# A two-layer hybrid decoder trunk: the low parts of the weight tiles by an accumulating transfer

## Chip, cores and metric

The kernel runs on one core of a Trainium2 chip. The metric is the device time of one execution in microseconds. Two runs of the kernel before took 1311.83 and 1311.68 us, median 1311.76 us.

## What is computed

A sequence of 16 meta tokens and 512 input tokens of width 1024 goes through two layers in float32. Each layer has a mixer (one input projection of 26 column tiles, three kinds of heads side by side, one output projection of 8 column tiles) and a gated MLP (an up projection of 44 column tiles, a causal convolution of width 3, a down projection). Cut to what matters here:

```python
for l in range(DEPTH):                      # DEPTH = 2
    h = h + hybrid_mixer(rmsnorm(h, norm_mix_g[l]), w_in[l], ..., w_out[l], cos, sin)
    h = h + conv_glu_ffn(rmsnorm(h, norm_ffn_g[l]), ffn_w_up[l], ffn_conv_w[l],
                         ffn_conv_b[l], ffn_w_down[l])
return rmsnorm(h, final_norm_g)[:, N_META:]
```

## The kernel before

The residual stream lives in on-chip memory with features on partitions: `hT` is 128 x 8 x 528 (8 feature tiles, 528 tokens). Tokens are worked in two halves of 264 (256 to 258 in parts of the last layer).

Every projection is done with split operands. A float32 value is cut into a high part, rounded to the matmul's own float type, and a low part, the difference. For one column tile of a weight and one token half, `product` (L234) issues for each of the 8 contraction tiles (7 in some down projections) three products into one accumulator: high weight by high activation, high weight by low activation, low weight by high activation. That is 24 products per half. The activations are split by `split` (L304: ACT rounds, VectorE subtracts).

The weights come as a stream of 204 tiles, listed in `units` (L181 to L201) in the order of their use. A tile is 128 x 1024 float32, 512 KB. `fetch` (L205) has SP load it into a `raw` buffer, of which there are three. `prep` (L214) makes the parts: ACT rounds `raw` into `wh` (L222), VectorE subtracts `wh` from `raw` into `wl` (L223), and then the load of the tile two places on is issued (L226). `wh` and `wl` have four buffers each (`wpool`, L91). `pop` (L228) is called when the work on tile i begins and prepares tile i + 3. The parts of the first four tiles are made by code of their own at the start (`cut`, `hi`, `lo`, L974 to L991), half tile by half tile in places.

`run_units` (L245) walks through the tiles of a projection. Most tiles are worked alone: both token halves, then the next tile. At some places four tiles form a block that is worked token half by token half: first halves of all four, then second halves of all four, so that the second half of the inputs can be late. The blocks are the first four tiles of each input projection, both halves of the 8 tiles of each output projection, the first four of the first up group of each layer, and the 8 tiles of each layer's last down group.

The order on TensorE (PE) and SP is the order of the code, written by hand. ACT, VectorE (DVE) and GpSimd (POOL) are ordered by a scheduler that estimates when each instruction can go; every engine then works its list strictly in that order. The mixers' own products are put between the projection products by generators with estimated distances (`tick`, L128). POOL does only small memsets: the pads of new tiles, among them the first two columns of each up projection tile (L882).

Names in rows: `mm` are the accumulators of projections, `mx` those of mixers and norms; `xh`, `xl` and `ah`, `al` are the parts of activations; L305 and L306 are `split`; L320 and L316 take squares for a norm; L884 and L886 move an up projection's result out of the accumulator; L894 is its convolution, L901 a sigmoid, L855 a residual add.

Of the kernel before, what the change touches and what calls it, by code (L numbers as in the profile page):

```python
# [9 lines left out]
F32 = mybir.dt.float32  # L10
F32R = mybir.dt.float32r
I32 = mybir.dt.int32
AF = mybir.ActivationFunctionType
# [21 lines left out]
# distances, in us of the PE's work, between dependent products of the mixers and norms  # L35
# [28 lines left out]
# columns of the packed masks  # L64
# [5 lines left out]
# columns of the packed per-layer parameters  # L70
# [6 lines left out]
C_LAM, C_LB = 0, 2 * DEPTH        # of the parameters that are worked on first  # L77
NPRE = C_LB + 4 * DEPTH

# columns of the packed float constants  # L80
# [5 lines left out]
def hybrid_trunk_kernel(ctx, tc, x, w_in, w_out, w_up, w_down, par, pre_in, lru_w, kon, msk, rope, out):  # L86
# [21 lines left out]
    # Estimated PE time, for the distance between dependent products of a mixer.  # L108
    clk = [0.0]
    live = []          # [generator, earliest clock, key]  # L110
# [103 lines left out]
    def prep(upto):  # L214
        while n_prep[0] <= min(upto, len(units) - 1):
            i = n_prep[0]
            fetch(i)
            r, kn = raws.pop(i)
            wh = wpool.tile([P, KD * P], F32R, tag="wh", name=nm("wh"))
            wl = wpool.tile([P, KD * P], F32R, tag="wl", name=nm("wl"))  # L220
            n = kn * P
            S.copy(wh[:, 0:n], r[:, 0:n])  # L222
            V.tensor_tensor(wl[:, 0:n], r[:, 0:n], wh[:, 0:n].bitcast(F32), op=ALU.subtract)  # L223
            ready[i] = (wh, wl)
            n_prep[0] += 1
            fetch(i + 2)  # L226
# [18 lines left out]
    def run_units(todo, xs, halves, ks=None, first=0, last=0, between=None, late=0, joint=0):  # L245
        """todo: (needs, evac(i, t0, n, ps), after()) per unit. The first `first` and the last
        `last` units go token half by token half; the last `late` of the contraction tiles come
        after the others of all of the first units' first half."""
# [60 lines left out]
    accs = {}  # L309

    def norm_sq(k, t0, n, apart=False):
        """Adds the squares of one tile of h to the sums of its token half; those of the last may stay apart."""
        if k == 0 or apart and k == KD - 1:
            a = half("acc", 3) if k == 0 else half("hs")
            accs.setdefault(t0, []).append(a)
            S.activation(a[:, 0:n], hT[:, k, t0:t0 + n], AF.Square)  # L316
            return
        a = accs[t0][0]
        sq = half("hs")
        S.activation(sq[:, 0:n], hT[:, k, t0:t0 + n], AF.Square)  # L320
        V.tensor_tensor(a[:, 0:n], a[:, 0:n], sq[:, 0:n], op=ALU.add)

    def warm(n):
        """Keeps the array busy while it has nothing else to do: its clock rises with its use."""
        if n:
            ps = mx()
            for _ in range(n):
                PE.matmul(ps[:, 0:P], ones, ones, start=True, stop=True)  # L328

    def rstd(terms, n):  # L330
        """1 / sqrt of the mean square of n tokens, worked out with the tokens on partitions."""
        m = 2 if n <= 2 * P else 3
        w = n // m
        ps = mx()
        for a, t in enumerate(terms):
            for i in range(m):
                mm(ps[0:w, 8 * i + a:8 * i + a + 1], t[:, i * w:(i + 1) * w], mean0[:, 0:1])
        ss, sd, rs = (big("sm", 9, (P, 20)) for _ in range(3))
        V.tensor_reduce(ss[0:w, 0:m], ps[0:w, 0:8 * m].rearrange("p (i a) -> p i a", a=8)[:, :, 0:len(terms)],
                        axis=AX.X, op=ALU.add)  # L340
        S.activation(sd[0:w, 0:m], ss[0:w, 0:m], AF.Sqrt, bias=eps[0:w], scale=1.0)
        V.reciprocal(rs[0:w, 0:m], sd[0:w, 0:m])
        dg = half("dg", 1)
        V.tensor_tensor(dg[0:w, 0:n].rearrange("p (i t) -> p i t", t=w), ident[0:w, 0:w].unsqueeze(1).to_broadcast([w, m, w]),
                        rs[0:w, 0:m].unsqueeze(2).to_broadcast([w, m, w]), op=ALU.mult)
        return dg, w

    def spread(dgw, n):
        """The factors of the tokens, the same on every partition."""
        dg, w = dgw  # L350
        ps = mx()
        mm(ps[:, 0:n], ones[0:w, :], dg[0:w, 0:n])
        return ps[:, 0:n]
# [23 lines left out]
    def pieces(t0, n):  # L377
        """Splits a token range at chunk bounds: (first chunk, chunks, offset in the chunk, tokens, start)."""
# [23 lines left out]
    def hgrn_evac(l, h, d):  # L402
# [7 lines left out]
        def q(i, t0, n, ps):  # L410
            sg = half("hs")
            S.activation(sg[:, 0:n], ps[:, 0:n], AF.Sigmoid)
            # the factor 1 - lb of k rides on q: both meet only in products over the same feature
# [11 lines left out]
    # Scores of a chunk, sum_d q_t k_s prod_{s<r<=t} f_r, level by level: for blocks of h tokens,  # L425
    # A holds q times the decay from the start of its block and B k times the decay to the end of
    # its block (both products of factors in [0, 1]), and T the decay over whole blocks. Neighbour
    # blocks 2i, 2i+1 meet as A x B; two levels at a time share one stationary B.
    def hgrn(l, h, d, on):
# [15 lines left out]
        def blocks(x, n, hb, which):  # L445
            """The even (0) or odd (1) ones of each chunk's first 2n blocks of hb tokens."""
            return (x[:, :, 0:2 * n * hb].rearrange("p c (n two h) -> p c n two h", two=2, h=hb)[:, :, :, which, :])
# [4 lines left out]
        def grow(x, n, hb, t, which):  # L452
            """x of the even / odd blocks times the decay over their odd / even neighbours."""
# [10 lines left out]
        def put(cs, k, src, n, hb, m):  # L464
            """Keeps what the mask allows of the scores of the odd ones of 2n blocks of hb tokens."""
# [15 lines left out]
        # levels 2 and 4  # L481
# [27 lines left out]
        # levels 8 and 16  # L509
# [20 lines left out]
        # levels 32 and 64; the last block of 32 has 16 tokens  # L530
# [36 lines left out]
        # tokens on partitions: the sums of the norm are over the free axis, and the factors per partition  # L567
# [155 lines left out]
    def lru(l, j, xp, on):  # L723
# [16 lines left out]
        # with u = -log(a) / 2 and h = tanh(u): a = 2 / (1 + h) - 1, sqrt(1 - a^2) = 2 sqrt(h) / (1 + h)  # L740
# [38 lines left out]
    def layer(l):  # L779
# [71 lines left out]
        # output projection and residual, then the second norm  # L851
# [13 lines left out]
        # gated MLP  # L865
# [5 lines left out]
        def up_pair(j):  # L871
            us = {}

            def ev(key, m):
                """Keeps the product u, and starts the convolution with its last tap."""
# [76 lines left out]
    with tc.manual_schedule(engines={mybir.EngineType.PE, mybir.EngineType.SP}):  # L952
# [5 lines left out]
        # the first call loads the table of the square root, which holds the squares too  # L958
# [15 lines left out]
        def cut(i):  # L974
            """Starts the split of weight tile i; hi and lo go half by half."""
# [219 lines left out]
```

## Time and profile before

| | |
|---|---|
| median of two runs | 1311.76 us |
| span of the profiled execution | 1310.1 us |
| PE busy | 1295.4 us |
| VectorE busy | 836.7 us |
| ACT busy | 652.9 us |
| POOL busy | 9.3 us |
| transfers, share of the 16 DMA engines | 27.2% in the loads' queue |

The profile shows one execution. Its span runs from the first to the last instruction; the times of the two runs are 1.6 to 1.7 us longer than that span. Busy times of engines overlap. A busy share tells how much an engine works, not what it makes others wait for; that is read from the waits and from the chain of work that ended last, which is followed back from the last instruction to what released each step. Line numbers are those of the kernel before; those of the kernel after are higher by one from L224 on.

### The profile page before, as it was taken

The page shows a single profiled execution, that of the slowest core. Times are in us where ns is not written, and L with a number is a line of the kernel's source. Part 1 is how long each engine was busy: PE and PEld are TensorE (multiplying, and loading weights), DVE is VectorE, ACT ScalarE, POOL GpSimd, SP SyncE. Part 2 cuts the span into 40 slices and gives each one's busy share as a digit, 9 for nine tenths or more (in the row PEclk, how much of TensorE's full clock was granted, in tenths as well). Part 3 has the DMA queues.
Part 4 walks back from the last instruction along what each step waited for, and adds up shares of the span by engine and source line. Part 5 has one row for each costly group of instructions (what it writes and reads, how often), then busy time and mean ns, then how long its engine had stood idle before and what let it go on. Part 6 is the DMA issues. An engine that isn't in the chain of part 4 may idle for free.

```text
span 1310.1 us, 25008 instructions
## 1 busy us (share of the span) xinstructions
PE 1295.4 (99%) x10312; PEld 1271.0 (97%) x10312; DVE 836.7 (64%) x1588; ACT 652.9 (50%) x1314; POOL 9.3 (1%) x99
## 2 busy tenths in 40 slices
PE   9999999999999999999999999999999999999997
PEld 9999999999999999999999999999999899989997
DVE  7987676477654664466488767754866456636654
ACT  6665555256533552455366645553655245425541
POOL 0000000000000000000000000000000000000000
PEclk8999999999999999999999999999999999999999
DMA  5222312223332323323222222122332333332221
GB/s 194 97 78 63 98 57 74 81 66 113 89 90 97 97 74 103 94 86 98 65 88 75 65 66 97 62 68 66 104 106 86 94 97 92 85 113 87 91 65 66
DMA packets 36082, 114.22 MB, mean 87 GB/s; under 512 B 3840, under 2 KB 8448, under 8 KB 35968
## 3 DMA queue, kind: packets, MB, share of 16 engines
q1 hardware_dynamic: 34816, 110.46, 27.2%
q10 hardware_dynamic: 1152, 2.16, 0.5%
q8 instruction: 81, 1.33, 0.4%
q14 instruction: 33, 0.27, 0.1%
HBM read 110.51 MB, written 2.10 MB: 86 GB/s over the span
## 4 chain that ended last, share of the span: by engine, by line
PE 93%; DVE 3%; ACT 2%; DMA 1%; issue 0%; SPq 0%; DVEq 0%; ACTq 0%
PE mm L115 85%; PE mx L115 7%; PE mx L122 1%; DVE t L443 1%; DMA raw<-in_w_in_dram 0%; DVE sc L467 0%; DMA mk<-in_msk_dram 0%; DVE t L746 0%; ACT sc L550 0%; DVE wl L223 0%; DVE t L933 0%; ACT wh L222 0%; DVE hT L855 0%; DVE rr L443 0%; PE mx L328 0%
## 5 line engine op out<-in xcount | busy, mean ns | idle before, releaser
L115 PE MATMUL mm<-xh,wh 128*128 128x264 f32 (+2 forms) x2240 | 648.0, 289 | 0.0
L115 PE MATMUL mm<-xh,wl 128*128 128x264 f32 (+2 forms) x2240 | 634.9, 283 | 0.0
L115 PE MATMUL mm<-xl,wh 128*128 128x264 f32 (+2 forms) x2240 | 634.3, 283 | 0.0
L115 PEld LDWEIGHTS mm<-xh,wh 128*128 128x128 f32 x2240 | 422.6, 189 | 2.4 <-issue 2.0
L115 PEld LDWEIGHTS mm<-xl,wh 128*128 128x128 f32 x2240 | 422.1, 188 | 2.6 <-issue 1.9
L115 PEld LDWEIGHTS mm<-xh,wl 128*128 128x128 f32 x2240 | 422.7, 189 | 0.1
L223 DVE TENSOR_TENSOR wl<-raw,wh 128x1024 fp32r<-128x1024 f32 (+1 forms) x200 | 240.4, 1203 | 170.7 <-ACT wh L222 170.1
L222 ACT CAST wh<-raw 128x1024 fp32r<-128x1024 f32 (+1 forms) x200 | 206.6, 1033 | 245.0 <-PE mm L115 244.9
L115 PE MATMUL mm<-ah,wh 128*128 128x264 f32 (+3 forms) x848 | 253.9, 299 | 0.0
L115 PE MATMUL mm<-al,wh 128*128 128x264 f32 (+3 forms) x848 | 252.8, 298 | 0.0
L115 PE MATMUL mm<-ah,wl 128*128 128x264 f32 (+3 forms) x848 | 252.4, 298 | 0.0
L115 PEld LDWEIGHTS mm<-al,wh 128*128 128x128 f32 x848 | 159.6, 188 | 5.0
L115 PEld LDWEIGHTS mm<-ah,wl 128*128 128x128 f32 x848 | 159.7, 188 | 4.9
L115 PEld LDWEIGHTS mm<-ah,wh 128*128 128x128 f32 x848 | 159.6, 188 | 4.9
L894 DVE SCALAR_TENSOR_TENSOR t<-t,pr,t 128x528 f32<-128x528 f32 (+1 forms) x176 | 133.1, 757 | 3.0
L886 ACT ACTIVATE t<-mm,pr 128x264 f32<-128x264 f32 (+1 forms) x176 | 101.2, 575 | 0.0
L884 ACT COPY t<-mm 128x264 f32<-128x264 f32 (+2 forms) x176 | 65.2, 371 | 56.8 <-PE mm L115 56.8
L776 DVE TENSOR_TENSOR hT<-hT,mm 128x264 f32<-128x264 f32 (+1 forms) x48 | 24.7, 515 | 76.6 <-PE mm L115 76.6
L901 ACT ACTIVATE t<-t 128x528 f32<-128x528 f32 (+1 forms) x44 | 28.1, 639 | 86.3 <-DVE t L894 86.2
L855 DVE TENSOR_TENSOR hT<-hT,mm 128x264 f32<-128x264 f32 (+2 forms) x64 | 26.3, 424 | 56.0 <-PE mm L115 56.0
L320 ACT ACTIVATE hs<-hT 128x264 f32<-128x264 f32 (+2 forms) x52 | 21.3, 419 | 60.0 <-DVE hT L855 58.5
L902 DVE TENSOR_TENSOR t<-t,t 128x528 f32<-128x528 f32 (+1 forms) x44 | 30.8, 701 | 31.2 <-ACT t L901 31.0
(189 smaller groups left out, 1058.5 us busy)
## 6 DMA issues: line engine op xcount, KB each, us to landing
raw<-in_w_up_dram SPq DMA_DIRECT2D x88, 512.0 KB, 3.6
raw<-in_w_in_dram SPq DMA_DIRECT2D x52, 512.0 KB, 3.6
raw<-in_w_down_dram SPq DMA_DIRECT2D x32, 448.0 KB, 3.3
raw<-in_w_out_dram SPq DMA_DIRECT2D x16, 512.0 KB, 3.6
raw<-in_w_down_dram SPq DMA_DIRECT2D x16, 512.0 KB, 3.6
hT<-in_x_dram SPq DMA_DIRECT2D x4, 528.0 KB, 5.6
t<-in_rope_dram ACTq DMA_DIRECT2D x8, 264.0 KB, 3.2
out_dram<-t SPq DMA_DIRECT2D x8, 256.0 KB, 2.2
```

The source lines that it names most:

```text
L115: PE.matmul(o, a, b, start=start, stop=stop)
L122: PE.transpose(o, a, ident[0:n, 0:n])
L222: S.copy(wh[:, 0:n], r[:, 0:n])
L223: V.tensor_tensor(wl[:, 0:n], r[:, 0:n], wh[:, 0:n].bitcast(F32), op=ALU.subtract)
L320: S.activation(sq[:, 0:n], hT[:, k, t0:t0 + n], AF.Square)
L776: V.tensor_tensor(hT[:, m, t0:t0 + n], hT[:, m, t0:t0 + n], ps[:, 0:n], op=ALU.add)
L855: V.tensor_tensor(hT[:, m, t0:t0 + n], hT[:, m, t0:t0 + n], ps[:, 0:n], op=ALU.add)
L884: S.copy(u[:, 2 + t0:2 + t0 + n], ps[:, 0:n])
L886: S.activation(c[:, o - c0:t0 + n - c0], ps[:, o - t0:n], AF.Identity, bias=pr[l][:, C_FB + m:C_FB + m + 1], scale=pr[l][:, w + 2:w + 3])
L894: V.scalar_tensor_tensor(c[:, 0:cn], u[:, i + c0:i + c0 + cn], pr[l][:, w + i:w + i + 1], c[:, 0:cn], op0=ALU.mult, op1=ALU.add)
L901: S.activation(sg[:, 0:cn], c[:, 0:cn], AF.Sigmoid)
L902: V.tensor_tensor(c[:, 0:cn], c[:, 0:cn], sg[:, 0:cn], op=ALU.mult)
```

## The change

In `prep`, VectorE's subtraction goes. ACT makes a second pass over the raw tile and writes it to `wl` negated, rounded by the type of `wl` as `wh` is. Then POOL issues a transfer from `raw` to `wl`, both in on-chip memory, that adds its source to what stands in the destination, so that `wl` ends as raw minus rounded raw. The diff also strips comments and docstrings, which changes no instruction.

```diff
             S.copy(wh[:, 0:n], r[:, 0:n])
-            V.tensor_tensor(wl[:, 0:n], r[:, 0:n], wh[:, 0:n].bitcast(F32), op=ALU.subtract)
+            S.activation(wl[:, 0:n], r[:, 0:n], AF.Copy, scale=-1.0)
+            G.dma_start(wl[:, 0:n], r[:, 0:n], accum_op=ALU.add)
             ready[i] = (wh, wl)
```

The first four tiles keep VectorE's subtraction. The order on PE and SP is the same as before, but what each waits for is not: PE's third product of a contraction tile now waits for the transfer, and a raw buffer may be loaded again only when the transfer that reads it has landed. On ACT, POOL and VectorE the scheduler has made a new order.

On ACT, just before the first singles of layer 0's input projection, the copies of the fifth and sixth tile stand like this before:

```order
L222 CAST wh_261<-raw_259 128x1024
L827 COPY t_318<-mm_448 128x264
L404 ACTIVATE t_321<-mm_449 128x264
L405 ACTIVATE t_322<-mm_449 128x264
L727 ACTIVATE t_642<-t_318,pr_78 128x528
L222 CAST wh_332<-raw_265 128x1024
```

and after:

```order
L222 CAST wh_261<-raw_259 128x1024
L828 COPY t_319<-mm_451 128x264
L405 ACTIVATE t_322<-mm_452 128x264
L406 ACTIVATE t_323<-mm_452 128x264
L728 ACTIVATE t_646<-t_319,pr_78 128x528
L223 ACTIVATE wl_262<-raw_259 128x1024
L413 ACTIVATE hs_600<-mm_575 128x264
L222 CAST wh_333<-raw_266 128x1024
```

The negated copy (L223) of the fifth tile stands behind four instructions that follow its rounding copy. On ACT at the change from layer 0's output projection to its up projection, the second and third tile of the up projection's first block are treated like this before (`xh` is the norm's rounding):

```order
L222 CAST wh_3270<-raw_3204 128x1024
L305 CAST xh<-hs_3402 128x264
L305 CAST xh<-hs_3406 128x264
L305 CAST xh<-hs_3410 128x264
L305 CAST xh<-hs_3414 128x264
L222 CAST wh_3305<-raw_3239 128x1024
```

and after:

```order
L222 CAST wh_3301<-raw_3234 128x1024
L306 CAST xh<-hs_3435 128x264
L306 CAST xh<-hs_3439 128x264
L306 CAST xh<-hs_3443 128x264
L306 CAST xh<-hs_3447 128x264
L223 ACTIVATE wl_3302<-raw_3234 128x1024
L222 CAST wh_3337<-raw_3270 128x1024
```

The second tile's negated copy comes after four of the norm's roundings, and the third tile's rounding copy one instruction later. POOL, where the up projection of layer 0 begins, has only memsets before:

```order
L882 MEMSET t_3532 128x2
L882 MEMSET t_3583 128x2
L882 MEMSET t_3653 128x2
L882 MEMSET t_3689 128x2
L882 MEMSET t_3857 128x2
```

and after, transfers (L224) with memsets between them:

```order
L224 DMA wl_3338<-raw_3270 128x1024
L224 DMA wl_3535<-raw_3306 128x1024
L883 MEMSET t_3618 128x2
L883 MEMSET t_3689 128x2
L883 MEMSET t_3726 128x2
L224 DMA wl_3572<-raw_3342 128x1024
L224 DMA wl_3624<-raw_3539 128x1024
```

POOL's queue is worked in this order, so a transfer goes when the memsets ahead of it have gone.

## Rows read from the trace of the kernel before

**Rows 1.** The page, part 1: busy time, share of the span, instructions.

```profile
PE 1295.4 (99%) x10312; PEld 1271.0 (97%) x10312; DVE 836.7 (64%) x1588; ACT 652.9 (50%) x1314; POOL 9.3 (1%) x99
```

**Rows 2.** The chain that ended last: shares by engine; pieces (start us, us, what).

```profile
PE 93%; DVE 3%; ACT 2%; DMA 1%; issue 0%; SPq 0%; DVEq 0%; ACTq 0%
...
281.70 0.87 PE mx L115 x12
...
284.59 367.89 PE mm L115 x3030
```

**Rows 3.** Waits of PE's weight loads: us in total, times, longest us.

```profile
PEld mx L115 <- DVE dg L344: 3.0, 2, 1.6
...
PEld mx L115 <- ACT bt L556: 1.3, 2, 0.8
```

**Rows 4.** Groups by line: busy us, mean ns of one | idle before.

```profile
L223 DVE TENSOR_TENSOR wl<-raw,wh 128x1024 fp32r<-128x1024 f32 (+1 forms) x200 | 240.4, 1203 | 170.7 <-ACT wh L222 170.1
L222 ACT CAST wh<-raw 128x1024 fp32r<-128x1024 f32 (+1 forms) x200 | 206.6, 1033 | 245.0 <-PE mm L115 244.9
...
L886 ACT ACTIVATE t<-mm,pr 128x264 f32<-128x264 f32 (+1 forms) x176 | 101.2, 575 | 0.0
L884 ACT COPY t<-mm 128x264 f32<-128x264 f32 (+2 forms) x176 | 65.2, 371 | 56.8 <-PE mm L115 56.8
```

**Rows 5.** Waits of all engines: us in total, times, longest us.

```profile
POOL t L882 <- DVE t L894: 269.9, 20, 95.8
```

**Rows 6.** Queues (packets, MB, share) and issues (KB each, median us to landing).

```profile
q1 hardware_dynamic: 34816, 110.46, 27.2%
...
raw<-in_w_up_dram SPq DMA_DIRECT2D x88, 512.0 KB, 3.6
...
hT<-in_x_dram SPq DMA_DIRECT2D x4, 528.0 KB, 5.6
```

**Rows 7.** Stretches: us; PE, PEld, DVE, ACT, POOL busy; clock, DMA share, GB/s.

```profile
10.00:14.30 4.30, 3.13 (x12) 2.93 (x13) 3.72 (x11) 3.40 (x9) 0.00 (x0) 0.52 1.06 391
...
60.00:180.00 120.00, 119.41 (x963) 116.64 (x962) 89.97 (x210) 67.09 (x163) 1.46 (x13) 1.00 0.26 79
```

**Rows 8.** Timeline, 34 to 41 us: start us, us, instruction, idle before.

```profile
34.33 1.05 ACT L222 CAST wh<-raw 128x1024 fp32r<-128x1024 f32 x1 [1.77 <-PE mm L115]
...
36.11 0.84 ACT L727 ACTIVATE t<-t,pr 128x528 f32<-128x528 f32 x1
...
40.55 1.06 ACT L222 CAST wh<-raw 128x1024 fp32r<-128x1024 f32 x1 [1.43 <-PE mm L115]
```

**Rows 9.** Timeline, 243 to 254 us.

```profile
243.11 1.05 ACT L222 CAST wh<-raw 128x1024 fp32r<-128x1024 f32 x1 [1.84 <-PE mm L115]
...
245.45 0.33 SPq L210 DMA_DIRECT2D raw<-in_w_out_dram  x1
...
251.90 1.05 ACT L222 CAST wh<-raw 128x1024 fp32r<-128x1024 f32 x1 [1.55 <-PE mm L115]
...
252.85 0.42 ACT L320 ACTIVATE hs<-hT 128x264 f32<-128x264 f32 x1
```

**Rows 10.** Timeline, 270 to 280 us.

```profile
270.67 1.05 ACT L222 CAST wh<-raw 128x1024 fp32r<-128x1024 f32 x1 [2.00 <-PE mm L115]
271.62 1.35 ACT L305 CAST xh<-hs 128x264 fp32r<-128x264 f32 x4
...
276.47 0.28 PE L115 MATMUL mm<-xh,wh 128*128 128x264 f32 x1
```

**Rows 11.** Timeline of ACT, 290 to 312 us.

```profile
292.49 1.05 ACT L222 CAST wh<-raw 128x1024 fp32r<-128x1024 f32 x1 [1.26 <-PE mm L115]
...
295.41 1.05 ACT L222 CAST wh<-raw 128x1024 fp32r<-128x1024 f32 x1 [1.12 <-PE mm L115]
...
298.52 0.65 ACT L901 ACTIVATE t<-t 128x528 f32<-128x528 f32 x1
```

## The prediction, made before the change was run

> **What bounds the kernel now.** I read the busy shares first [rows 1]: TensorE (PE) works 1295.4 of 1310.1 us, VectorE (DVE) 836.7, ScalarE (ACT) 652.9, GpSimd (POOL) 9.3. Then the chain of work that ended last [rows 2]: 93% PE, and its longest unbroken piece is 3030 products in 367.89 us. That is 0.1214 us a product, so a weight tile's half of the tokens (8 contraction tiles by 3 products) lasts 24 x 0.1214 = 2.91 us and a whole tile 5.83 us. Then the waits of PE's weight loads [rows 3]: the longest for other engines come to 3.0 and 1.3 us in all. PE is idle for 14.7 us in total, so an edit that only relieves VectorE has at most about 15 us to win, and the edit's cost is whatever new waiting it puts in front of PE. The question is therefore not how busy the engines are but when a tile's low part is there.
>
> **What goes and what comes.** The subtraction is 200 x 1203 ns = 240.4 us of VectorE [rows 4]; it goes, and VectorE falls to about 596 us. It is not what PE waits for, so I credit nothing; the bounds are 0 and 5 us, the waits of rows 3 together with a little of what stands on DVE in the chain. In its place ACT makes a second pass over the tile, priced as the rounding copy of the same shape: 200 x 1033 ns = 207 us [rows 4], ACT to about 860 us or 66%. In the mixers of layer 0 ACT has 67 of 120 us [rows 7], to which some 14 tiles add 15; VectorE there has 90 and loses 17. These two I set against each other, with 5 us either way. POOL issues 200 transfers. Its in-order queue holds the memsets of the new tiles in between, so a late memset would hold a transfer; in the trace they wait for their buffers up to 95.8 us [rows 5], but go as soon as these are free, well before they are used, so nothing is charged.
>
> The third part decides: an accumulating transfer of 512 KB within the on-chip memory. Call L the time from its issue to its landing. No such transfer is in the trace. The lower end is a plain load of the same bytes, 3.6 us [rows 6]. The upper end is two such loads one after the other, 7.2 us, since source and destination both have to be fetched; the first loads of the program, which run several at a time, land after 5.6 us for about the same bytes. Between the ends: the loads' queue takes 27.2% of 1310.1 us [rows 6], 356 us, for 211 loads' worth of bytes (110.46 MB / 0.524 MB), so 1.69 us of the DMA engines per load. So a landing of 3.6 is 1.9 fixed and 1.69 moving; with both operands moving it is 1.9 + 3.4 = 5.3 alone, and 7.0 if a weight load shares the engines. I take the middle, L = 6.2, and stretch a load that runs beside it by 0.85.
>
> **Where L is covered and where not.** There are four buffers for the low parts. In a run of single tiles the buffer for tile i+3 comes free as tile i starts, so three tiles, 17.5 us, lie between release and need. ACT needs some 3.1 of these (copy, an eviction, negated copy), so L could be 14 before PE waits; nothing is lost there. Where four tiles are worked token half by token half, all four buffers are held until the second halves end, one every 2.91 us, and the next tile is needed three halves, 8.7 us, after the first release. Each such place, read from the ACT timeline:
>
> Start [rows 8]. The fifth tile's copy begins at 34.33; four evictions follow, the last ending at 36.95, and the negated copy stands behind them in ACT's new order, ending at 38.0. The block ends at 40.55 (where the copy of tile eight is released), the low part is read by the third product, so at 40.8. Cover 2.8, loss L - 2.8 = 3.4 us.
>
> Second block of the output projection [rows 9]. The release of its first buffer is at 243.11; copy and negated copy end at 245.2; the need is at 251.9, so up to L = 6.7 it is covered. The fourth tile is another matter. There are three buffers for the raw tiles, and its load was issued at 245.45, when the first tile's subtraction had read the buffer. Now the buffer is held until the accumulate has landed: 245.2 + L, load 3.6 + 0.85, copy 1.05, a square 0.42, negated copy 1.05, and L again: 252.2 + 2L, against a need at 251.9 + 3 x 2.91 + 0.2 = 260.9. Loss 2L - 8.7 = 3.7 us. On SP only further loads stand behind the waiting one.
>
> First block of the up projection [rows 2, 10]. The second tile's copy starts at 270.67, the four roundings of the norm (1.35) now stand between it and the negated copy, which ends at 274.0; the block starts at 276.47, so the need is at 276.47 + 2.91 + 0.2 = 279.6. Cover 5.6, loss 0.6 us. The third and fourth are needed more than 2.91 us apart, since PE breaks off at 281.70 for the norm's products and comes back to long work only at 284.59; by the same steps they are covered somewhat longer, to about 6.
>
> First singles after it [rows 11]. The first has its copy at 292.49 and its negated copy, behind an eviction (0.37 + 0.58 [rows 4]), ends at 295.35; the block ends three halves after 292.49, need at 301.4: covered to 6.1. The second: its copy at 295.41, then an eviction, a table load, a sigmoid that ends at 299.2, the next tile's copy (1.05), an eviction (0.95) and a rounding of the sigmoid's shape (0.65); with these the negated copy ends at about 302.5, need 5.83 later at 307.3. Cover 4.8, loss 1.4 us.
>
> The last three places together lose 5.7 us. They come once with layer 0's output projection, once where layer 0's down projection meets layer 1's input projection, and once with layer 1's output projection: 17.1. The last down projection has a second block only: 3.7. With the start, 17.1 + 3.7 + 3.4 = 24.2 us. The profiled execution would span 1310.1 + 24.2 = 1334.3; the two timed runs (median 1311.76) lie 1.7 above the span of before, so 1336. Per microsecond of L the loss changes by 15 (one at the start, 2 x 4 in the second blocks, 3 + 3 in the other places): at 5.3 it is 12 us, at 7.2 about 39. At 3.6 only the start is left, 0.8.
>
> What the loss leaves out is PE's clock. It is granted at 1.00 (2.4 GHz) from 60 to 180 us, where PE hardly idles, and at 0.52, near the 1.2 GHz level, from 10.0 to 14.3, where PE works 3.13 of 4.30 us [rows 7]. Whether waits of 3 us bring it down I can't tell; at each of 11 places the lower level for as long as that stretch would add 11 x 2.1 = 23 us, an upper bound that I leave to the range.
>
> A word on the transfer's price from elsewhere. The Trainium skill, "DMA: Bandwidth & Descriptors", section "Anatomy of one DMA", gives a GpSimd-issued transfer 2.0 us plus its bytes at 436 GB/s; with the bytes of both operands that is an estimate of 4.4 us, by which the start would lose 1.6 us, the second blocks 0.1 each, and the time would be 1314. The trace puts a load of 512 KB at 3.6 us, where the same formula gives 3.2, so it is a little hopeful here. The Trainium skill, the same page, section "Issuing engines are not separate DMA queues", says that all issuers share the same 16 engines, which speaks against this change, and the first loads, 5.6 us for about the same bytes while others run [rows 6], agree: by it L is nearer to 7.0, the time 1348.
>
> **The rivals.**
> Hidden: every block is covered, only the start loses. For it: the DMA engines are at 27% [rows 6], there is much room. Against: two operands, a load at the same time. Time 1311.8 + 1.5 = 1313. This is the case on the other side, not slower; it holds up to L = 4.35, where the second blocks begin to lose.
> Rate: the accumulate is far slower than its bytes. Raw buffers then set the pace of the singles too: load 3.6 + two copies 2.1 + L may not exceed 17.5 us, so from L = 11.8 each of some 150 singles costs (L - 11.8) / 3 more. At L = 10 only the blocks lose, 15 x 3.8 = 57 more than at 6.2: 1393; at 14 it is 1336 + 117 + 110 = 1563. For it: an addition inside a transfer occurs nowhere in this trace. Against: nothing.
> Relief: VectorE's 240 us shorten the mixers' chains by more than ACT's copies lengthen them, with L hidden. DVE is 3% of the chain [rows 2], but PE's own waits leave 5 us at most in the middle: 1307.
> ACT binds: the negated copies delay evictions and the norm's roundings. It has 34% spare, and PE waited for it 1.3 us [rows 3]. It would add 5 to 15 us to the forecast.
>
> **Chances.** Block losses, L from 4.35 to 8.5: 0.65, 1313 to 1371, of which 0.32 lies under 1338 (L under 6.3). Hidden 0.15, rate 0.15, relief 0.03, ACT 0.02. Two per cent, 26 us, is about what a measurement here can tell from no change, so the line is at 1338: within it 0.32 + 0.15 + 0.02 of relief = 0.49; slower 0.33 + 0.15 + 0.02 = 0.50; faster 0.01, the rest of relief with a larger gain than I can find. The range takes in all of the hidden case and of the block losses and leaves out relief and the slower two thirds of the rate case (L over 10.4), some 0.13 in all: 1312 to 1400.
>
> **What will show it.** The low part's transfers with a median landing between 5.3 and 7.0; PE's weight loads waiting for that transfer, in groups of some 3 us, at 40, 255 to 310, 640 to 700, 910 to 960 and near 1290, and nowhere in the singles; a raw load in the second block issued about 6 us later after its predecessor than before; VectorE near 596 us, ACT near 860. A landing under 4.35 or over 8.5, or PE waiting in the middle of the up projection, would make the forecast wrong.

## The result, and the profile after

Two runs of the kernel after took 1350.77 and 1359.78 us, median 1355.28; the ratio to the kernel before is 1.033, with a 95% interval of 1.025 to 1.041. It is slower by 43.5 us. The forecast was 1336 with a range of 1312 to 1400: the size is 19 us short, and the side was hardly claimed, since slower had a chance of 0.50 and no change 0.49. Most of this document is on where those 19 us are and on a sum that came out right in part by luck.

The page of the kernel after, part 1, answers to [rows 1]:

```profile
PE 1307.8 (97%) x10312; PEld 1278.3 (95%) x10312; DVE 616.5 (46%) x1388; ACT 832.8 (62%) x1514; POOL 180.7 (13%) x299
```

The span is 1348.8 us, so PE is idle for 41.0 us against 14.7 before. The idle time grew by 26.3 us, PE's busy time by 12.4, though it runs the same 10312 products. Both have to be explained.

The groups by line of the kernel after (busy us, mean ns of one | idle before it), to [rows 4]:

```profile
L222 ACT CAST wh<-raw 128x1024 fp32r<-128x1024 f32 (+1 forms) x200 | 206.6, 1033 | 247.2 <-PE mm L115 195.6
L224 POOL DMA_DIRECT2D wl<-raw x200 | 172.6, 863 | 1102.5 <-ACT wl L223 650.2
...
L223 ACT ACTIVATE wl<-raw 128x1024 fp32r<-128x1024 f32 (+1 forms) x200 | 207.9, 1041 | 0.0
```

ACT's second pass takes the time that was put down for it (1041 ns for 1033). POOL works 863 ns to issue one transfer, 172.6 us in all, which the forecast had not counted; it is no extra term, since the landing times below count from the start of the issue.

The queues of the kernel after (packets, MB, share of the 16 DMA engines) and its issues (KB, median us to landing), to [rows 6], and the landings of the low parts' transfers alone:

```profile
q0 software_dynamic: 28800, 102.77, 42.4%
q1 hardware_dynamic: 34816, 110.46, 26.4%
...
wl<-raw POOLq DMA_DIRECT2D x168, 512.0 KB, 5.5
raw<-in_w_up_dram SPq DMA_DIRECT2D x88, 512.0 KB, 5.1
```

```profile
DMA to landing us min/median/max: 4.4/5.5/8.7
```

An accumulate lands 5.5 us after its issue in the median. It takes 42.4% of 1348.8 us for 196 tiles' worth of bytes (102.77 MB / 0.524 MB), 2.92 us of the DMA engines, 1.7 times a load's 1.69. A load of the up projection takes 5.1 us instead of 3.6 beside them.

The median is not what PE meets. By the landings in the trace, the 22 transfers that ran with no load and no other transfer beside them took 4.6 us in the median, and the 146 that overlapped another accumulating transfer 5.9. The 16 that PE waited for took 6.7 in the median, 4.5 to 8.7.

The waits of PE's weight loads in the kernel after (us in total, times, longest us), to [rows 3]:

```profile
PEld mm L115 <- DMA wl<-raw: 24.9, 16, 4.0
...
PEld mx L115 <- DVE dg L345: 3.4, 2, 2.0
PEld mx L115 <- issue: 2.9, 3, 2.2
```

The new wait is first in the list with 24.9 us; the forecast's sum was 24.2. Single waits in PE's timeline (start us, us, instruction, idle before it) show where it stands: the start, a second block of layer 0's output projection, the first block of layer 1's input projection, and the two longest.

```profile
43.42 0.19 PEld L115 LDWEIGHTS mm<-xh,wl 128*128 128x128 f32 x1 [2.24 <-DMA wl<-raw]
...
265.69 0.19 PEld L115 LDWEIGHTS mm<-ah,wl 128*128 128x128 f32 x1 [1.48 <-DMA wl<-raw]
...
270.06 0.19 PEld L115 LDWEIGHTS mm<-ah,wl 128*128 128x128 f32 x1 [1.41 <-DMA wl<-raw]
...
682.65 0.19 PEld L115 LDWEIGHTS mm<-xh,wl 128*128 128x128 f32 x1 [1.48 <-DMA wl<-raw]
...
931.11 0.29 PEld L115 LDWEIGHTS mm<-ah,wl 128*128 128x128 f32 x1 [4.05 <-DMA wl<-raw]
...
955.12 0.29 PEld L115 LDWEIGHTS mm<-xh,wl 128*128 128x128 f32 x1 [3.18 <-DMA wl<-raw]
```

The last two of these matter twice. Stretches of the kernel after (us; PE, PEld, DVE, ACT, POOL busy; clock; DMA share; GB/s), one of the long run of single tiles and then a few around these two waits:

```profile
330.00:620.00 290.00, 290.00 (x2391) 290.00 (x2391) 109.07 (x161) 181.59 (x289) 48.31 (x89) 1.00 0.83 184
```

```profile
926.00:930.00 4.00, 1.27 (x11) 1.06 (x9) 0.85 (x2) 0.42 (x1) 0.00 (x0) 1.00 0.90 216
930.00:934.00 4.00, 2.89 (x13) 2.89 (x14) 0.00 (x0) 0.00 (x0) 0.00 (x0) 0.55 0.52 140
934.00:938.00 4.00, 4.00 (x24) 4.00 (x23) 0.85 (x2) 1.22 (x2) 0.00 (x0) 0.59 0.03 8
938.00:942.00 4.00, 4.00 (x38) 4.00 (x37) 1.08 (x4) 2.79 (x5) 0.00 (x0) 1.00 0.00 0
...
958.00:962.00 4.00, 4.00 (x21) 4.00 (x20) 0.75 (x3) 0.30 (x1) 0.00 (x0) 0.50 1.01 209
```

In the single tiles PE works 290.00 of 290.00 us with the DMA engines at 83%: nothing is lost there. At the end of the wait of 4.05 us the granted clock falls to the lower level (1.2 GHz), and a full window of 4 us there holds 21 to 24 products, against 38 in the one where the clock is back at 1.00. PE counts as busy in it; this is how busy time grows without more work. The mean clock of the two executions (core, span, clock), the kernel before in the second fence:

```profile
core 0: 1348.8 us, clock 0.989
```

```profile
core 0: 1310.1 us, clock 0.995
```

1.1% of 1348.8 us is 14.8, 0.5% of 1310.1 is 6.6: the clock took 8.2 us more. With the 24.9 us of waits that makes 33.1 of the 38.7 us by which the span grew. The second timed run had a clock of 0.984 and a span of 1357.8, so most of the 9 us between the two runs is clock as well (21.7 against 14.8 us by the same sum).

### The profile page after: what moved, and what is told of

Read it like the earlier page. It is cut to its first block, busy times and chain, and to the rows that moved or that the text cites. A ratio compares the mean times of both kernels' runs of the same rounds, so it can differ in the third digit from the quotient of the medians.

```text
span 1348.8 us, 25400 instructions
## 1 busy us (share of the span) xinstructions
PE 1307.8 (97%) x10312; PEld 1278.3 (95%) x10312; DVE 616.5 (46%) x1388; ACT 832.8 (62%) x1514; POOL 180.7 (13%) x299
## 3 DMA queue, kind: packets, MB, share of 16 engines
q0 software_dynamic: 28800, 102.77, 42.4%
## 4 chain that ended last, share of the span: by engine, by line
PE 77%; issue 10%; DMA 7%; DVE 3%; ACT 1%; POOL 1%; SPq 0%; POOLq 0%; DVEq 0%; ACTq 0%
PE mm L115 68%; PE mx L115 7%; DMA wl<-raw 4%; DMA raw<-in_w_in_dram 1%; PE mx L122 1%; DMA raw<-in_w_up_dram 1%; DMA raw<-in_w_down_dram 1%; POOL wl L224 1%; DMA mk<-in_msk_dram 0%; DVE sc L468 0%; DVE t L444 0%; DVE t L747 0%; ACT sc L551 0%; DVE t L934 0%; ACT wh L222 0%
## 5 line engine op out<-in xcount | busy, mean ns | idle before, releaser
L222 ACT CAST wh<-raw 128x1024 fp32r<-128x1024 f32 (+1 forms) x200 | 206.6, 1033 | 247.2 <-PE mm L115 195.6
L224 POOL DMA_DIRECT2D wl<-raw x200 | 172.6, 863 | 1102.5 <-ACT wl L223 650.2
L115 PE MATMUL mm<-ah,wl 128*128 128x264 f32 (+3 forms) x848 | 254.9, 301 | 14.0 <-DMA wl<-raw 13.9
L223 ACT ACTIVATE wl<-raw 128x1024 fp32r<-128x1024 f32 (+1 forms) x200 | 207.9, 1041 | 0.0
L115 PE MATMUL mx<-rr,t 128*112 128x168 f32 (+2 forms) x320 | 48.5, 299 | 3.1 <-issue 2.0
```

The lines of the kernel that those rows point to most:

```text
L115: PE.matmul(o, a, b, start=start, stop=stop)
L223: S.activation(wl[:, 0:n], r[:, 0:n], AF.Copy, scale=-1.0)
L224: G.dma_start(wl[:, 0:n], r[:, 0:n], accum_op=ALU.add)
```

## The experiments

Each was timed in rounds beside the kernel before, whose median was 1311.6 to 1312.0 us throughout. To say where time went, I cut PE's timeline at the first product of each stage and took each stage's length less that of before. "Output" is the sum over the two output projections and the two last down projections, "norm side" that over the two input projections (with the mixers) and the two first up groups, that is, the places behind a norm. The long stretches between, 483 us, are equal to before within 0.1 us in every kernel. A low clock is inside these numbers, and they are of one profiled execution each, while the medians are of two to ten runs.

| kernel | median us | ratio, 95% | output | norm side |
|---|---|---|---|---|
| after | 1355.3 | 1.025 to 1.041 | +19.3 | +18.8 |
| ACT's pass, no transfer | 1331.1 | 1.0133 to 1.0163 | +0.5 | +18.8 |
| copies put first in the order | 1356.5 | 1.0316 to 1.0352 | +13.6 | +29.7 |
| four raw buffers | 1340.9 | 1.0204 to 1.0234 | +9.6 | +19.2 |
| change in the singles only | 1314.1 | 1.0006 to 1.0025 | -0.1 | +1.6 |
| change at the 44 tiles only | 1349.0 | 1.0256 to 1.0290 | +21.3 | +19.0 |
| VectorE negates | 1348.0 | 1.0239 to 1.0296 | +4.6 | +30.1 |
| ACT's pass at the 44, no transfer | 1324.4 | 1.0079 to 1.0109 | +0.4 | +13.6 |
| smaller pools (control) | 1352.3 | 1.0289 to 1.0320 | +20.9 | +20.2 |
| transfer in two halves | 1354.9 | 1.0299 to 1.0355 | +18.6 | +25.3 |
| four raw buffers, VectorE negates | 1349.1 | 1.0267 to 1.0298 | +4.4 | +31.1 |
| change at the output blocks only | 1330.0 | 1.0125 to 1.0159 | +16.6 | 0.0 |
| change at the norm side only | 1329.1 | 1.0117 to 1.0156 | +0.5 | +17.5 |

**ACT's pass without the transfer.**

```diff
             S.activation(wl[:, 0:n], r[:, 0:n], AF.Copy, scale=-1.0)
-            G.dma_start(wl[:, 0:n], r[:, 0:n], accum_op=ALU.add)
+            V.tensor_tensor(wl[:, 0:n], r[:, 0:n], wh[:, 0:n].bitcast(F32), op=ALU.subtract)
```

> Keeps ACT's negated copy of all 200 tiles, but has VectorE subtract as before the change (its subtraction overwrites the negated copy); no transfer. Theory (PE waits for the landing of the transfers at the changes between blocks): the extra pass adds at most 1.05 us to a path that had over 6 us of cover, so 1312 to 1316 us and PE's weight loads wait for wl less than 1 us in all. Rival (ACT's second pass and its longer queue are the cost): most of the loss stays, over 1335 us.

It took 1331.1 us: a miss, 19 us lost without any transfer. The waits of PE's weight loads say where:

```profile
PEld mx L115 <- issue: 9.7, 8, 2.0
PEld mx L122 <- PE mx L122: 3.9, 4, 1.1
...
PEld mm L115 <- DVE wl L224: 1.8, 3, 1.3
```

Nearly all of these are products of the mixers and norms (`mx`), not of the weights (`mm`). In the output blocks, where the forecast had most of its loss, nothing is lost. My theory's time falls with this. But the run is no clean price of ACT's pass: VectorE's subtraction writes the same buffer as the pass and waits for it, which the changed kernel doesn't have. The run on 44 tiles below shows what that does.

**Copies and transfer put first in the order.** The negated copy, the transfer and the rounding copy, now in this order, get a high priority in the scheduler.

```diff
-            S.copy(wh[:, 0:n], r[:, 0:n])
-            S.activation(wl[:, 0:n], r[:, 0:n], AF.Copy, scale=-1.0)
-            G.dma_start(wl[:, 0:n], r[:, 0:n], accum_op=ALU.add)
+            with tc.high_priority(400):
+                S.activation(wl[:, 0:n], r[:, 0:n], AF.Copy, scale=-1.0)
+                G.dma_start(wl[:, 0:n], r[:, 0:n], accum_op=ALU.add)
+                S.copy(wh[:, 0:n], r[:, 0:n])
```

> As the change, but the negated copy, the transfer and the rounding copy have high priority in the scheduler, so that on ACT the two passes over a tile stand next to each other, without evictions and roundings of the norm between them. Theory: only the places where something stood between get earlier, the start (by 1.9 us), the first up block (by 1.35 us) and the first singles; PE's waits for wl fall from 25 us to 16 to 20 us, the time to 1338 to 1350 us. Rival (ACT's queue is the cost): below 1325 us. Rival (the DMA engines' rate): no change, 1350 to 1360 us.

The waits for the transfer halved to 12.1 us, below the theory's 16 to 20, but the time was 1356.5: a miss. It lies in the second rival's range, though not for its reason, since the waits did change. PE now waited for what had been put behind:

```profile
PEld mm L115 <- DMA wl<-raw: 12.1, 11, 3.5
PEld mm L115 <- ACT xh L307: 7.3, 3, 3.1
PEld mx L115 <- issue: 4.5, 3, 3.9
...
PEld mx L115 <- ACT rr L488: 3.7, 1, 3.7
```

`xh` is the norm's rounding, `rr` a mixer's copy. In this order the tiles are earlier and the norms and mixers later; the output stages win 6 us by it and the norm side loses 11.

**Four raw buffers.** To find the room, two other pools get one buffer less each; the control has these smaller pools alone.

```diff
-TB = 10
+TB = 9
...
-    def half(tag="hs", bufs=4):
+    def half(tag="hs", bufs=3):
...
-            r = wpool.tile([P, KD * P], F32, tag="raw", name=nm("raw"), bufs=3)
+            r = wpool.tile([P, KD * P], F32, tag="raw", name=nm("raw"), bufs=4)
```

> As the change, with four raw buffers instead of three, so that the fourth tile of a second block is loaded before the first one's transfer lands (two smaller pools give up a buffer each to make room). Theory: the waits for the fourth tile of the four second blocks (1.4, 1.4, 4.1 and 1.9 us) go, and with the longest of them the stretch at the lower clock behind it: 1335 to 1344 us, waits for wl 14 to 18 us. Rivals (ACT, DMA rate): no change, 1350 to 1360 us.

> The changed kernel with the two pools as small as the run with four raw buffers needed them (nine instead of ten, three instead of four), but still three raw buffers. Theory (the fourth raw buffer, not the smaller pools and the new order that comes with them, won the 14 us): 1350 to 1360 us, waits for the transfer 22 to 27 us. Rival (the order made the difference): 1338 to 1346 us.

Four raw buffers took 1340.9 us, the control 1352.3: both times as the theory said, with waits for the transfer of 18.2 us, just over its bound, and 25.8. The output stages lose 9.6 us instead of 20.9, the norm side is in sum as before. So some 11 us come from the raw buffer being held until the transfer lands: 7.6 us fewer waits, and the rest mostly clock (0.992 against 0.989). The timelines of ACT, SP and POOL in the kernel after show the hold itself, in the second block of layer 0's output projection:

```profile
251.76 0.86 POOL L224 DMA_DIRECT2D wl<-raw  x1 [13.46 <-ACT wl L223]
...
256.38 0.33 SPq L210 DMA_DIRECT2D raw<-in_w_out_dram  x1
...
261.94 1.05 ACT L222 CAST wh<-raw 128x1024 fp32r<-128x1024 f32 x1 [4.30 <-DMA raw<-in_w_out_dram]
263.22 1.04 ACT L223 ACTIVATE wl<-raw 128x1024 fp32r<-128x1024 f32 x1
...
264.56 0.86 POOL L224 DMA_DIRECT2D wl<-raw  x1 [6.07 <-ACT wl L223]
```

The first tile's transfer goes at 251.76, and the load into its buffer is issued 4.6 us later, when it has landed. The fourth tile's copy waits for that load until 261.94, where before ACT had waited only for PE [rows 9]; its transfer goes at 264.56, and PE waits for it until 270.06, 5.5 us later. With four raw buffers the copy that stands there waits for PE again:

```profile
261.82 1.05 ACT L222 CAST wh<-raw 128x1024 fp32r<-128x1024 f32 x1 [0.60 <-PE mm L115]
```

The held buffer also costs in a mixer, which the forecast had not seen. ACT and then PE in the kernel after, where layer 1's input projection goes over to single tiles:

```profile
708.72 1.04 ACT L222 CAST wh<-raw 128x1024 fp32r<-128x1024 f32 x1 [3.77 <-DMA raw<-in_w_in_dram]
709.67 0.43 ACT L472 COPY rr<-t 128x280 f32<-128x280 f32 x1
...
710.17 0.98 PEld L115 LDWEIGHTS mx<-rr,t 128*112 128x112 f32 x7 [2.23 <-issue]
```

A transfer landed at 702.80, the load into its buffer was issued at 702.85 and landed at 708.70, and ACT's rounding copy waited for it. The mixer's copy `rr`, whose input VectorE had finished at 705.39, stands behind that copy in ACT's list, and PE waits 2.23 us; "issue" means that the trace names no releaser, so that it is `rr` is read from the names and the times. With four raw buffers the rounding copy at this place waits for PE alone, and PE has no such wait there:

```profile
706.88 1.05 ACT L222 CAST wh<-raw 128x1024 fp32r<-128x1024 f32 x1 [0.61 <-PE mm L115]
```

**The change in the singles only, and at the changes only.** The 44 tiles are the fifth to seventh of the program, and at each change of stage the last tile of the first token-half block, the whole second block, and after a norm the next block and three singles.

```diff
+CHANGE = frozenset([4, 5, 6, *range(29, 41), *range(97, 109), *range(131, 143), *range(199, 204)])
...
+            if i in CHANGE:
+                V.tensor_tensor(wl[:, 0:n], r[:, 0:n], wh[:, 0:n].bitcast(F32), op=ALU.subtract)
+            else:
                 S.activation(wl[:, 0:n], r[:, 0:n], AF.Copy, scale=-1.0)
                 G.dma_start(wl[:, 0:n], r[:, 0:n], accum_op=ALU.add)
```

The second kernel has `not in` for `in`.

> The change for the 156 tiles that are worked alone with their predecessors alone; the 44 tiles at the changes between blocks keep VectorE's subtraction. Theory: all transfers have three tiles, 17.5 us, of cover: 1308 to 1315 us, PE waits for wl under 2 us. Rivals (ACT's pass, or the DMA engines' rate): some 156/200 of the loss stays, 1335 to 1350 us.

> The negated copy and the transfer are made only for the 44 tiles at block changes; the 156 tiles of the singles keep VectorE's subtraction. Theory (all of the transfer's loss arises at the block changes): the run with the transfer in the singles alone lost 2 us, so this one has nearly all of the 43 us of the full change: 1340 to 1357 us, waits of PE's weight loads for the transfer 20 to 27 us in total, the long up-projection singles unchanged. Rival (a good part of the loss comes from ACT's longer list through the mixers, which has 156 copies fewer here): 1322 to 1336 us with the same waits for the transfer.

The singles alone cost 2 us (1314.1), with 156 of the 200 transfers and no wait of PE for them; it also frees VectorE of 170 us, and no gain shows. The 44 tiles alone cost 37 us (1349.0). Both are as their theories had it. Waits of the second:

```profile
PEld mm L116 <- DMA wl<-raw: 26.6, 15, 5.3
```

The two losses, 2.1 and 37.1, make 39, about the whole change (40.4 in the control, 43.5 in the first two runs).

**VectorE makes the negated copy.**

```diff
-            S.activation(wl[:, 0:n], r[:, 0:n], AF.Copy, scale=-1.0)
+            V.tensor_scalar(wl[:, 0:n], r[:, 0:n], -1.0, None, op0=ALU.mult)
```

> VectorE instead of ACT makes the negated copy, for all 200 tiles; the transfer is kept. Theory (the transfer's landing time and the raw buffer that it holds make the loss; ACT's second pass only where it stands behind other work on ACT): waits for the transfer 16 to 26 us in total and 1338 to 1356 us, ACT back near 650 us. Rival (ACT's second pass makes a loss of its own of some 19 us, as the run without a transfer had): 1325 to 1337 us, most of it gone from the input projections and the first up group.

1348.0 us, in the theory's range, but not by its reasons: the waits for the transfer fell to 13.9, under its bound, and the output stages lose only 4.6. There the copy now runs beside ACT's:

```profile
265.74 1.05 ACT L222 CAST wh<-raw 128x1024 fp32r<-128x1024 f32 x1 [3.70 <-DMA raw<-in_w_out_dram]
...
265.76 0.69 DVE L223 TENSOR_SCALAR wl<-raw 128x1024 fp32r<-128x1024 f32 x1 [1.91 <-DMA raw<-in_w_out_dram]
...
266.98 0.86 POOL L224 DMA_DIRECT2D wl<-raw  x1 [4.64 <-DVE wl L223]
```

From the copy's start to the transfer's issue it is 1.24 us here and 2.62 in the kernel after (261.94 to 264.56); by that the blocks are nearly in time. On the norm side the loss is 30.1 instead of some 20, since VectorE makes the norm's low parts there and the negated copies stand behind them: for the second tile of layer 0's up projection ACT's copy starts at 283.48 and VectorE's at 289.66. Its transfer lands 4.5 us after the issue, and PE still waits 3.28 us; at the same place in the other two blocks behind a norm it waits 3.31 and 3.54.

**ACT's pass at the 44 tiles, no transfer anywhere.** ACT's negated copy is overwritten by VectorE's subtraction, as in the first run.

```diff
             else:
                 S.activation(wl[:, 0:n], r[:, 0:n], AF.Copy, scale=-1.0)
-                G.dma_start(wl[:, 0:n], r[:, 0:n], accum_op=ALU.add)
+                V.tensor_tensor(wl[:, 0:n], r[:, 0:n], wh[:, 0:n].bitcast(F32), op=ALU.subtract)
```

> No transfer anywhere. At the 44 tiles at block changes ACT makes the negated copy, and VectorE then subtracts over it as before; the other 156 tiles are made as in the kernel before. It computes the same as before; ACT's copy there is overwritten. Theory (ACT's pass costs at the block changes little by itself; the 19 us of the run with the pass on all tiles were lost in the mixers' chains): 1311 to 1318 us. Rival (the pass itself makes the blocks late): 1322 to 1332 us, about what the pass on all tiles cost.

1324.4 us, in the rival's range: 44 copies of 1.05 us on ACT, with VectorE's subtractions behind them, lose 12.5 us, nearly all of it behind norms. ACT's timeline, where layer 1's up projection begins, and VectorE's in the next fence:

```profile
923.07 1.05 ACT L223 CAST wh<-raw 128x1024 fp32r<-128x1024 f32 x1 [0.96 <-PE mm L116]
924.02 0.40 ACT L310 CAST xh<-hs 128x258 fp32r<-128x258 f32 x1
924.33 1.05 ACT L227 ACTIVATE wl<-raw 128x1024 fp32r<-128x1024 f32 x1
925.29 0.70 ACT L310 CAST xh<-hs 128x258 fp32r<-128x258 f32 x2
```

```profile
921.84 1.23 DVE L228 TENSOR_TENSOR wl<-raw,wh 128x1024 fp32r<-128x1024 f32 x1 [0.96 <-ACT wl L227]
...
930.80 3.49 DVE L228 TENSOR_TENSOR wl<-raw,wh 128x1024 fp32r<-128x1024 f32 x3
934.20 1.33 DVE L326 TENSOR_TENSOR acc<-acc,hs 128x256 f32<-128x256 f32 x3
```

ACT alternates between copies (L223, L227) and the norm's roundings (L310) without a gap. VectorE's subtraction can go only after ACT's negated copy of the same tile (the wait at 921.84). The subtractions that follow gather on VectorE, and the three sums `acc` of the second token half's norm stand behind them until 934.20. PE waits for these sums:

```profile
935.65 0.52 PEld L116 LDWEIGHTS mx<-mean,acc 128*128 128x128 f32 x4 [1.61 <-issue]
```

Here too no releaser is named; that it is `acc`, which ends at 935.53, is read from the names and the times.

This chain is one of this kernel, not of the change. In the kernel after, VectorE has no subtraction there, and the last of the three sums is done at 951.04:

```profile
950.62 0.42 DVE L322 TENSOR_TENSOR acc<-acc,hs 128x256 f32<-128x256 f32 x1
```

PE then waits from 951.94 to 955.12 for the transfer, and its products on `acc` follow with no wait of their own. So the 12.5 us are no price of ACT's pass in the change. A pass into a buffer of its own, for which VectorE need not wait, would give that price; it was not run.

**The transfer in two halves.**

```diff
-            G.dma_start(wl[:, 0:n], r[:, 0:n], accum_op=ALU.add)
+            for c0, c1 in ((0, n // 2), (n // 2, n)):
+                G.dma_start(wl[:, c0:c1], r[:, c0:c1], accum_op=ALU.add)
```

> The changed kernel with each accumulating transfer cut into two halves of 256 KB, issued one after the other; PE's first third product needs the first half only. Theory (waits go by the time from issue to landing): the first half has about 1.5 us less to move (half of the 2.9 us of the DMA engines per transfer), so each of the some 15 waits for the transfer is up to 1.5 us shorter, waits for it 10 to 18 us in total, 1334 to 1350 us. Rival (what an accumulate takes is mostly fixed, and POOL's second issue of 0.86 us and the raw buffer, held as long or longer, eat the rest): waits 22 to 32 us, 1350 to 1365 us.

1354.9 us: no gain. Of this kernel the landings:

```profile
DMA to landing us min/median/max: 3.1/4.8/9.3
```

This is over both halves. By the single landings, the first halves take 3.7 us in the median (3.1 to 7.1), 1.8 less than a whole transfer, as the theory had it. But the second halves, issued some 0.54 us later, land 6.6 us after the first one's issue, 1.1 later than a whole transfer, and the raw buffer is held as long. PE needs the second half 12 products after the first, 1.46 us, so a tile gains 0.4 us at most (an estimate: 5.5 against 6.6 - 1.46). The trace names the transfer for 5.4 us of waits only, but 15 waits before a `wl` load, 21.9 us in all, end within 0.2 us of the landing of a half, so the transfer's waits are 21.9 against 24.9. The theory's first step held; the rival's second issue and longer hold ate the gain, the time is in the rival's range, and the output stages (18.6) are where they were.

**Four raw buffers and VectorE's copy together.** Both edits above.

> Four raw buffers (in the smaller pools) and VectorE's negated copy together; the transfer is kept for all tiles. Theory (the held raw buffer and ACT's longer list are two causes, which add up): the 11 us of the one and the 4 to 5 us of the other off the 1352 of the smaller pools, 1334 to 1340 us, with waits for the transfer under 10 us. Rival (what either takes away is the same waiting, and VectorE's pass costs in the mixers): 1341 to 1350 us.

1349.1 us, with waits for the transfer of 16.9: the two do not add up. In the output stages VectorE's copy alone had taken the loss to 4.6, and a fourth raw buffer leaves it at 4.4; the norm side loses 31.1.

**The output blocks and the norm side apart.** The change of the 44 tiles is cut into 20 (`range(29, 34)`, `range(97, 102)`, `range(131, 136)`, `range(199, 204)`) and the other 24.

> ACT's negated copy and the transfer only for 20 tiles: the last tile of the first block and the whole second block of each output projection and of each last down projection (five each). All other tiles keep VectorE's subtraction. Theory (in these blocks the transfer's landing decides, and it costs there what the run on all 44 tiles lost in these stages, 21 us): 1328 to 1337 us, the loss in these four stages, waits for the transfer 14 to 20 us. Rival (a late block there is made good by work that is ready behind it, or the loss needs late tiles on both sides): 1313 to 1324 us.

> ACT's negated copy and the transfer only for the other 24 tiles of the 44: the fifth to seventh at the start and the first block with the next three singles of the first up projection group of each layer and of layer 1's input projection. All other tiles keep VectorE's subtraction. Theory (behind a norm it is ACT's pass among the roundings, not the transfer, that costs; the pass on all 44 tiles without a transfer lost 13 us there): 1322 to 1331 us, waits for the transfer 5 to 10 us. Rival (these places are late only because the output blocks before them are): 1312 to 1319 us.

1330.0 and 1329.1 us, both in the theory's range; the first loses only in the output stages, the second only on the norm side. Waits for the transfer of the first, and in the second fence of the second:

```profile
PEld mm L116 <- DMA wl<-raw: 14.0, 8, 5.2
```

```profile
PEld mm L116 <- DMA wl<-raw: 7.9, 6, 2.6
```

In the first, 14.0 us of waits and 2.7 of clock (0.993 of 1326.8 us) make the 16.7 by which its span grew. In the second it is 7.9 of waits, 8.0 of clock (0.989 of 1328.1) and a mixer's wait of 2.6 at 702 us, against 18.0. No wait for the norm's sums grew, so the second theory's reason, ACT's pass among the roundings and not the transfer, is not what the trace shows.

So the loss has three parts that nearly add: 18.2 us in the output blocks, 17.2 behind the norms, 2.1 in the rest, 37.5 of the 40 to 43.

## Why the prediction was right or wrong

**What bounds it, and that relief is worth nothing: right, as far as tested.** A kernel with 170 us less on VectorE (the singles alone) was 2 us slower, not faster. VectorE itself fell to 616.5 us where 596 was forecast: rows of neighbouring instructions overlap by some 0.1 us, so 200 of them take 20 us less of the busy time than the sum of their group. ACT rose to 832.8 and not 860 in the same way.

**Nothing is lost in the singles: right but for 2 us.** 156 transfers cost 2 us, with no wait of PE for them.

**The places: right.** PE waits at 43, 265 to 290, 635 to 683, 903 to 987 and 1297 to 1323, and nowhere else for this transfer. Of the singles behind the blocks, forecast at 1.4 us three times, only one shows a wait, of 0.34 us at 987.

**The sum of 24.2 us: the mechanism right, the total (24.9) in part by luck.** L was taken as 6.2. The median of all is 5.5, by which my own slope gives 24.2 - 15 x 0.7 = 13.7; but the landings that PE waited for took 6.7, so L was no bad price where it counts. The terms are off in both directions: the start 2.2 us, where I had 3.4; the four second blocks 12.6, where I had 14.8; the first blocks of the output stages 3.7, where I had none; the three first blocks behind a norm 6.0, where I had 0.6 each; the singles behind them 0.3, where I had 4.2. The chain of 2L and a load was right in kind, and four raw buffers took half of the loss in these stages away; its load took 5.6 us (256.38 to 261.94) where I had 4.45, and each transfer leaves 0.3 us after its negated copy.

By the Trainium skill, "DMA: Bandwidth & Descriptors", section "Anatomy of one DMA", the estimate was 4.4 us. That is this kernel's shortest landing and near the 4.6 of the transfers that ran alone; it is 1.1 us under the median and 2.3 under what PE waited for, so the measurement decides against it as a price here.

**"These two I set against each other", with 5 us either way: nothing was put down, and 4.7 us came.** PE has three longer waits in the mixers that the kernel before lacks, 1.22 us each at 59.5 and 64.4 and 2.23 at 710.2. The longest is not ACT's added work but its order: a mixer's copy stands behind a rounding copy that waits for a held raw buffer. I had looked at what stands behind the waiting load on SP, and not at what stands on ACT behind the copy that needs this load. The trace puts the other two down to VectorE's and PE's own work, and they were not followed further. What ACT's second pass costs by itself stays open: the two runs that keep it without the transfer (19 and 12.5 us) make VectorE wait for it, which the change does not.

**The clock, left to the range: it should have been a term.** Two of the waits, 4.05 and 3.18 us, are followed by the lower level, 8.2 us over the whole span. The windows of 905 to 945 and 945 to 990 us have 0.91 and 0.89, so they lose 3.6 and 5.0 us, where the estimate was 2.1 a place; the waits of 2.3 us and less had none in this execution.

The 19 us between 1336 and 1355 are then some 8 of clock and 5.6 of other waits (38.7 - 24.9 - 8.2), of which 4.7 are those in the mixers, and the rest is the second timed run, which lies 9 us above the first and raises the median by 4.5.

## What to carry to other kernels

An engine that is never waited for has no price to save: ask instead what the replacement holds, and for how long. A transfer in place of an instruction holds its source buffer until it lands, so at a change of stage its latency counts twice, once for the tile and once for the tile that reuses the buffer. And where a copy may wait for a load, read what stands behind it on its own engine, which works its list in order. A control that leaves a part of a change out can add a wait of its own: compare its chain with that of the changed kernel before its loss is called a price.

## What was not expected of the hardware

An accumulating transfer within the on-chip memory takes 4.6 us in the median when it runs alone and 5.9 beside another one, up to 8.7; those that PE waits for are among the slow ones, 6.7 in the median. The first 256 KB of a split transfer land in 3.7 us and 512 KB in 5.5, which gives some 2 us fixed and 3.5 moving (an estimate from these two), close to the forecast's 1.9 and 3.4. Each issue takes 0.86 us of POOL. The granted clock fell to the lower level as waits of PE of 3 to 4 us ended, and was back at 1.00 after some 7 and 10 us. In other kernels it also fell after shorter ones: 2.23 us at 42.8 with the change on the norm side only, 1.61 at 935.7 with ACT's pass at the 44 tiles. It makes most of the 9 us between the two runs, where a kernel without these waits stays within 1311.25 to 1313.14 in seven.
